# Weight parts at other byte offsets in a fp32 decoder trunk: a ring of six places and a cycle of eight wide offsets

## The chip, the cores and the metric

The kernel runs on one core of one Trainium2 chip. Its metric is the device time of one execution in microseconds (us). A comparison of this kernel with another one can tell a difference of about 2% from no change.

The engines are named as the profile names them: PE multiplies matrices (PEld is its loading of the stationary operand, LDWEIGHTS), ACT and DVE work elementwise, POOL here mostly issues DMAs that add to their target, and SP issues the other DMAs.

## The reference

One sequence of 512 tokens with 1024 features goes through two layers, in fp32. Layer 0 mixes with a gated DeltaNet (6 heads of 128, in chunks), layer 1 with sliding-window attention (12 query heads, 2 shared key/value heads); both attend to 256 memory tokens as well. Each layer ends in a SwiGLU of width 2816:

```
x = x + concat([mix_out, mem_o]) @ w_out[layer]
x = x + swiglu(rms_norm(x, ln_ffn[layer]), w_gate_up[layer], w_down[layer])

def swiglu(h, w_gate_up, w_down):
    gu = h @ w_gate_up
    return (jax.nn.silu(gu[..., :D_FF]) * gu[..., D_FF:]) @ w_down
```

After the last layer comes one more RMS norm. Most of the arithmetic is in these matrix products: the input projections, w_out, w_gate_up and w_down.

## The kernel before

**Three products for one.** Every fp32 operand of a large product is split into a high part (rounded to the matmul's fp32r form by a copy on ACT) and a low part (the rest, by a subtraction on DVE): `split`, lines 176 to 178. Then `mm3` (lines 206 to 212) issues three matmuls for each 128 rows of contraction: high weight by high activation, high weight by low activation, low weight by high activation. The weight is the stationary operand, the activation the moving one, with 512 or 256 columns (tokens).

**Where the parts lie.** `parts` (lines 190 and 191) takes a pair of tiles, `whi` for the high and `wlo` for the low part, from a pool with three buffers of each. A tile has 1024 + 64 elements of 4 bytes in each partition; SPARE is the 64. `weight` (lines 193 to 204) loads a raw weight (`wraw`) and puts both parts at element 0 of such a pair; these are the *wide* weights, up to 1024 elements long. In the built program all these tiles and all activations begin at the same remainder modulo 256 bytes, so a part's offset in its tile is also its offset from the moving operand, modulo 256.

**The quarters and the ring.** Most of w_gate_up is multiplied with seven products of half size in place of eight (a Strassen-like scheme). `quarters` (lines 1005 to 1052) does one such group for a pair of column tiles; each call of `product` (lines 1020 to 1025) takes one of the seven half weights (512 elements), splits it on ACT and DVE, and multiplies it with 256 columns by 4 times `mm3`, which is 12 matmuls. `held` copies a finished sum out of its PSUM bank (the `fs` tiles, 256 elements on ACT); sums of finished products go to `fu` and `fg` tiles on DVE. The half weights live in a *ring* of six places (lines 893 to 900): three pairs of tiles, each cut into two halves of 512 elements, and used in turn, so the two halves of one pair are neighbours in the order of use. Before the change the halves lie at elements 16 to 527 and 528 to 1039 of the tile (SHIFT is 16). There are two stretches of ten quarters in each layer's `ffn`, 70 products each, four stretches in all; `places` is emptied at the start of each, so each begins a new round of the ring with its first product.

**What orders the work.** The order on each engine is set when the program is built, by a scheduler that follows the dependences between tiles. A split into a place of the ring waits until the matmuls that read what it overwrites are done; where two areas of a tile overlap in a single element, that counts as the same data. Each engine then works through its instructions in that order, and waits on semaphores.

Of the kernel before, what the change touches and what calls it, by code (L numbers as in the profile page):

```python
# [19 lines left out]
T = 512  # L20
# [7 lines left out]
FT = DFF // P  # L28
EPS = 1e-6
LINE = 64  # L30
SHIFT, SPARE = 16, 64
NEG = -1e30
BASE = 32
NB = P // BASE
# [54 lines left out]
class Builder:  # L89
    def __init__(self, tc, a):  # L90
        self.tc, self.nc, self.a = tc, tc.nc, a
        self.n = 0
        self.table, self.table_ins, self.table_users = None, None, []


# [97 lines left out]
    def weight(self, src, eng=None, raw=None, parts=1, pool=None, tags=("whi", "wlo"), bufs=3):  # L193

        raw = self.load(src) if raw is None else raw
        n = raw.shape[1]
        if pool is None:
            hi, lo = (x[:, :n] for x in self.parts())
        else:
            hi, lo = (self.t(pool, [P, D], F32R, t, bufs)[:, :n] for t in tags)  # L200
        for i in range(parts):
            s = slice(i * n // parts, (i + 1) * n // parts)
            self.split(raw[:, s], hi[:, s], lo[:, s], eng or self.weng)
        return hi, lo
# [665 lines left out]
    def ffn(self, fp, xp, layer, h, apool, rope=False):  # L870
# [3 lines left out]
        acts, sums, open_pairs, places = [], [], [], []  # L874
# [18 lines left out]
        def ring():  # L893

            if not places:
                for _ in range(3):
                    two = self.parts()
                    places.extend(tuple(x[:, SHIFT + i * T:SHIFT + (i + 1) * T] for x in two) for i in range(2))
            places.append(places.pop(0))
            return places[-1]  # L900

        def begin(f, up, by, tag, bufs, then):

            o = [self.t(fp, [P, T], F32, tag, bufs) for _ in range(2)]
            steps = self.quarters(fp, [col(f + i, up) for i in range(2)], sums, by, o, ring)
            next(steps)
            end()
            next(steps)
            open_pairs.append((steps, then, o))
            return o  # L910
# [13 lines left out]
        for f0, half in ((0, 12), (12, 10)):  # L924
# [16 lines left out]
            for m in range(tail):  # L941
                ps = self.bank("pj")
                for j in (0, 6):
                    n = min(6, half - j)
# [8 lines left out]
        if tail < KD:  # L953
# [9 lines left out]
            for t in parts:  # L963
                acc = self.acc[:, t]
                for m in range(tail, KD):
# [3 lines left out]
                    x = self.x[m][:, t]  # L969
# [301 lines left out]
```

## Time and profile before

| | |
|---|---|
| time, median of 2 runs | 1159.43 us (1157.88 to 1160.98) |
| time of the profiled execution | 1156.72 us |
| its span, first to last instruction | 1155.0 us |
| PE busy | 1131.5 us (98%) |
| DVE busy | 842.6 us (73%) |
| ACT busy | 631.7 us (55%) |
| POOL busy | 86.0 us (7%) |
| granted PE clock | 0.998 of full |

The span is what the profile's views divide up; 1.7 us of the execution's time lie around it. Matmuls overlap each other: a matmul of 256 columns shows a duration of about 0.28 us, but the next one begins about 0.12 us later. What counts for the time is this distance from one start to the next, here called the pitch, and not the duration.

### The profile page before, as it was taken

Reading aid. Unit: us, or ns where it says so; the run is one execution under the profiler, and the core shown is the slowest. Engines: PE = TensorE matmul, PEld = TensorE weight load, DVE = VectorE, ACT = ScalarE, POOL = GpSimd, SP = SyncE. Lnnn points to the kernel's source line nnn. Section 1 sums busy time; section 2 is a strip of 40 time slices with the busy share of each in tenths; the row PEclk is TensorE's granted clock in tenths of the full one; section 3 lists DMA queues with packets and bytes.
Section 4 is the critical chain, followed back from the end, with each engine's and each line's share of the span. In section 5 each row is a group of like instructions: output and inputs, shape, how many; then the busy total and the mean of one; then the engine's idle time right before and its main releaser. Section 6 shows DMA issues by size and latency. Waiting matters only on the chain.

```text
span 1155.0 us, 19665 instructions
## 1 busy us (share of the span) xinstructions
PE 1131.5 (98%) x7476; PEld 992.9 (86%) x7476; DVE 842.6 (73%) x1587; ACT 631.7 (55%) x1271; POOL 86.0 (7%) x97
## 2 busy tenths in 40 slices
PE   7999999999999999999999999999999999999996
PEld 6888778887899998899998777777899988999986
DVE  6754877767789987389866767859799843898754
ACT  7579563366556652256654547675566522566533
POOL 0310000000101100011100000010011100111000
PEclk9999999999999999999999999999999999999999
DMA  8434342225657744567723421144477733577232
GB/s 309 133 106 117 113 103 98 92 92 165 168 139 190 188 123 126 154 147 188 178 70 104 137 73 38 51 107 126 110 188 191 183 109 105 141 183 188 72 94 94
DMA packets 73971, 152.83 MB, mean 132 GB/s; under 512 B 17756, under 2 KB 18420, under 8 KB 73876
## 3 DMA queue, kind: packets, MB, share of 16 engines
q1 hardware_dynamic: 62356, 130.59, 36.2%
q0 software_dynamic: 11520, 20.98, 11.7%
q8 instruction: 59, 0.97, 0.4%
q14 instruction: 36, 0.29, 0.1%
HBM read 144.58 MB, written 6.96 MB: 131 GB/s over the span
## 4 chain that ended last, share of the span: by engine, by line
PE 85%; DVE 8%; ACT 3%; DMA 3%; issue 1%; SPq 0%; DVEq 0%; ACTq 0%
PE pj L154 40%; PE g L154 38%; PE sc L154 5%; DVE wlo L161 2%; ACT sm L142 1%; PE pt L158 1%; DMA wraw<-in_wout 1%; PE qk L154 1%; ACT whi L148 1%; PE g L158 1%; DVE l L164 1%; DMA wraw<-in_wmk 1%; DVE btmp L161 1%; DVE stats L778 1%; DVE big L161 1%
## 5 line engine op out<-in xcount | busy, mean ns | idle before, releaser
L148 ACT ACTIVATE whi<-wraw 128x512 fp32r<-128x512 f32 (+2 forms) x331 | 244.1, 745 | 256.1 <-PE pj L154 155.9
L161 DVE TENSOR_TENSOR wlo<-wraw,whi 128x512 fp32r<-128x512 f32 (+2 forms) x331 | 274.6, 839 | 104.6 <-ACT whi L148 98.6
L154 PE MATMUL pj<-h,whi 128*128 128x512 f32 (+1 forms) x676 | 266.5, 396 | 0.0
L154 PE MATMUL pj<-l,whi 128*128 128x512 f32 (+1 forms) x676 | 264.9, 392 | 0.5 <-DVE l L164 0.4
L154 PE MATMUL pj<-h,wlo 128*128 128x512 f32 (+1 forms) x676 | 264.3, 391 | 0.0
L154 PE MATMUL g<-T,whi 128*128 128x256 f32 x1280 | 230.2, 281 | 0.0
L154 PEld LDWEIGHTS g<-T,whi 128*128 128x128 f32 x1280 | 197.5, 190 | 1.7 <-DVE fu L164 1.7
L154 PE MATMUL g<-T,wlo 128*128 128x256 f32 x640 | 179.9, 281 | 0.0
L154 PEld LDWEIGHTS pj<-h,whi 128*128 128x128 f32 x676 | 126.8, 188 | 29.2 <-issue 3.6
L154 PEld LDWEIGHTS pj<-l,whi 128*128 128x128 f32 x676 | 127.2, 188 | 27.8 <-issue 1.8
L154 PEld LDWEIGHTS pj<-h,wlo 128*128 128x128 f32 x676 | 127.1, 188 | 25.6 <-issue 0.8
L154 PE MATMUL g<-l,whi 128*128 128x256 f32 (+1 forms) x508 | 146.1, 288 | 0.0
L154 PE MATMUL g<-h,whi 128*128 128x256 f32 (+1 forms) x508 | 146.0, 287 | 0.0
L154 PE MATMUL g<-h,wlo 128*128 128x256 f32 (+1 forms) x508 | 145.9, 287 | 0.0
L154 PEld LDWEIGHTS g<-T,wlo 128*128 128x128 f32 x640 | 120.2, 188 | 0.0
L154 PEld LDWEIGHTS g<-l,whi 128*128 128x128 f32 x508 | 97.4, 192 | 1.4 <-issue 0.2
L154 PEld LDWEIGHTS g<-h,whi 128*128 128x128 f32 x508 | 95.4, 188 | 1.2
L154 PEld LDWEIGHTS g<-h,wlo 128*128 128x128 f32 x508 | 95.4, 188 | 1.0
L1014 POOL DMA_DIRECT2D ws<-in_wgu x40 | 35.4, 884 | 700.9 <-ACT sq L151 244.5
L148 ACT ACTIVATE whi<-ws 128x512 fp32r<-128x512 f32 x80 | 50.5, 631 | 51.3 <-PE g L154 42.1
L161 DVE TENSOR_TENSOR fu<-pj,rstd 128x512 f32<-128x512 f32 (+1 forms) x34 | 22.4, 660 | 54.3 <-PE pj L154 54.3
L161 DVE TENSOR_TENSOR wlo<-ws,whi 128x512 fp32r<-128x512 f32 x80 | 54.9, 686 | 6.9 <-ACT whi L148 6.8
(345 smaller groups left out, 1617.2 us busy)
## 6 DMA issues: line engine op xcount, KB each, us to landing
wraw<-in_wgu SPq DMA_DIRECT2D x48, 512.0 KB, 4.3
ws<-in_wgu SPq DMA_DIRECT2D x80, 256.0 KB, 3.7
ws<-in_wgu POOLq DMA_DIRECT2D x80, 256.0 KB, 4.8
wraw<-in_wdn SPq DMA_DIRECT2D x48, 384.0 KB, 3.1
wraw<-in_win SPq DMA_DIRECT2D x26, 512.0 KB, 3.6
wraw<-in_wgu SPq DMA_DIRECT2D x40, 256.0 KB, 4.2
wraw<-in_wout SPq DMA_DIRECT2D x16, 512.0 KB, 3.7
wraw<-in_wdn SPq DMA_DIRECT2D x16, 256.0 KB, 2.7
```

The source lines that it names most:

```text
L142: ins = self.nc.scalar.activation(out, in_, func, **kw).ins
L148: self.copied = self.nc.scalar.activation(out, in_, AF.Copy, **kw).ins
L154: return self.nc.tensor.matmul(out, lhsT, rhs, start=start, stop=stop, skip_group_check=more).ins
L158: return self.nc.tensor.transpose(out, in_, self.ident[:k, :k]).ins
L161: return eng.tensor_tensor(out=out, in0=a, in1=b, op=op).ins
L164: self.nc.vector.scalar_tensor_tensor(out=out, in0=in0, scalar=scalar, in1=in1, op0=op0, op1=op1)
L778: nc.vector.tensor_reduce(out=mx[:, i:i + 2], in_=ps[b], op=ALU.max, axis=AX.X)
L1014: nc.gpsimd.dma_start(s1, a22, accum_op=ALU.add)
```

## The change

The ring's six places get six different offsets in place of 16 elements for all, and a wide weight gets one of eight offsets in turn in place of 0. Nothing else is changed: the same splits, matmuls and DMAs are there, in the same number, on tiles of the same size at the same addresses.

```
-SHIFT, SPARE = 16, 64
+NARROW, WIDE, SPARE = ((56, 44), (36, 54), (50, 58)), (0, 52, 44, 40, 36, 20, 12, 28), 64
...
         if pool is None:
-            hi, lo = (x[:, :n] for x in self.parts())
+            o = WIDE[self.wide % len(WIDE)]
+            self.wide += 1
+            hi, lo = (x[:, o:o + n] for x in self.parts())
...
-                for _ in range(3):
+                for shifts in NARROW:
                     two = self.parts()
-                    places.extend(tuple(x[:, SHIFT + i * T:SHIFT + (i + 1) * T] for x in two) for i in range(2))
+                    places.extend(tuple(x[:, o + i * T:o + (i + 1) * T] for x in two) for i, o in enumerate(shifts))
```

The offsets are in elements. 56, 44, 36, 54, 50 and 58 elements are 224, 176, 144, 216, 200 and 232 bytes; counted up to the next multiple of 256 they leave the 32, 80, 112, 40, 56 and 24 of the change's description, and the wide ones (0, 208, 176, 160, 144, 80, 48 and 112 bytes from the tile's start) leave 0, 48, 80, 96, 112, 176, 208 and 144. So no offset of the ring stays as it was (64 bytes), and a wide weight stays at 0 in one use of eight.

The two halves of the first pair now lie at elements 56 to 567 and 44 + 512 = 556 to 1067: elements 556 to 567 belong to both. The second pair lies at 36 to 547 and 566 to 1077, the third at 50 to 561 and 570 to 1081, without a common element. In what follows, place 0 and place 1 are the two halves of the first pair.

This changes the order of the program in the four stretches of quarters. The first product of a stretch on PE, before (`whi_651` and `wlo_652` are the first pair of the ring, `whi_653` and `wlo_654` the second; `h` and `T` tiles are activations, `g` tiles are PSUM banks; the first two rows end the product of place 0, the rest begins that of place 1):

```order
L154 MATMUL g_648_3287<-l_571_2907,whi_651_3290 128x256
L154 MATMUL g_648_3287<-h_570_2906,wlo_652_3291 128x256
L154 MATMUL g_650_3289<-T_610_3125,whi_651_3290 128x256 [waits Activation_49]
L154 MATMUL g_650_3289<-T_611_3126,whi_651_3290 128x256
L154 MATMUL g_650_3289<-T_610_3125,wlo_652_3291 128x256 [waits DVE_49]
L154 MATMUL g_650_3289<-T_620_3173,whi_651_3290 128x256
```

The same place on PE now:

```order
L155 MATMUL g_648_3287<-l_571_2907,whi_651_3290 128x256
L155 MATMUL g_648_3287<-h_570_2906,wlo_652_3291 128x256
L155 MATMUL g_650_3289<-T_610_3125,whi_651_3290 128x256 [waits Activation_49]
L155 MATMUL g_650_3289<-T_611_3126,whi_651_3290 128x256
L155 MATMUL g_649_3288<-h_577_2945,whi_653_3292 128x256
L155 MATMUL g_648_3287<-T_610_3125,whi_653_3292 128x256 [waits Activation_49]
L155 MATMUL g_648_3287<-T_611_3126,whi_653_3292 128x256
L155 MATMUL g_648_3287<-T_610_3125,wlo_654_3293 128x256 [waits DVE_49]
L155 MATMUL g_650_3289<-T_610_3125,wlo_652_3291 128x256 [waits DVE_49]
```

Between the first two matmuls of place 1 and its third stand four matmuls of the second pair. The first matmul of place 1 directly follows the last of place 0 in both orders.

On ACT, the splits into the ring at the start of the same stretch, before (`whi_655` is the third pair; the rows between them belong to gates and sums of the same stage):

```order
L148 ACTIVATE whi_651_3290<-wraw_644_3277 128x512 [waits DMAHW3_49,PE_49]
L148 ACTIVATE T_640_3269<-fu_638_3262 128x512 [waits DVE_49]
L148 ACTIVATE whi_651_3290<-ws_645_3279 128x512 [waits DMASW0_49]
L142 ACTIVATE fg_616_3162<-fg_616_3162 128x512 [waits DVE_49]
L148 ACTIVATE T_640_3269<-fu_639_3263 128x512 [waits DVE_49]
L148 ACTIVATE whi_653_3292<-wraw_644_3277 128x512 [waits DVE_49,PE_49]
```

The same splits now, from the split into the second pair on to the next use of place 0:

```order
L149 ACTIVATE whi_653_3292<-wraw_644_3277 128x512 [waits DVE_49,PE_49]
L149 ACTIVATE whi_653_3292<-wraw_644_3277 128x512
L143 ACTIVATE fg_626_3210<-fg_626_3210 128x512 [waits DVE_49]
L149 ACTIVATE whi_655_3294<-wraw_644_3277 128x512 [waits DVE_49,PE_49]
L149 ACTIVATE whi_655_3294<-ws_646_3280 128x512 [waits DMASW1_49]
L143 ACTIVATE fg_636_3258<-fg_636_3258 128x512 [waits DVE_49]
L149 ACTIVATE whi_651_3290<-ws_645_3279 128x512 [waits DMASW0_49,PE_49,Activation_49]
L149 ACTIVATE fs_657_3310<-g_648_3287 128x256 [waits PE_49]
L149 ACTIVATE whi_651_3290<-wraw_662_3395 128x512 [waits DMAHW4_49,DVE_49,PE_49]
```

The split into place 1 (from `ws_645`) stood third in the ring's order and waited for its DMA alone. Now it stands behind the splits into the other four places, and waits for PE: the matmul it waits for is the last that reads the high part of place 0. The next split into place 0 waits for PE and DVE again.

Later in the stretch the scheduler puts more matmuls between place 0 and place 1. On PE in the second round (`g_668` is the bank of place 1's product; the first row ends the product of place 0):

```order
L155 MATMUL g_666_3405<-h_570_2906,wlo_652_3291 128x256
L155 MATMUL g_648_3287<-T_610_3125,whi_653_3292 128x256 [waits DVE_49]
L155 MATMUL g_648_3287<-T_611_3126,whi_653_3292 128x256
L155 MATMUL g_648_3287<-T_610_3125,wlo_654_3293 128x256
L155 MATMUL g_648_3287<-T_620_3173,whi_653_3292 128x256
L155 MATMUL g_648_3287<-T_621_3174,whi_653_3292 128x256
L155 MATMUL g_648_3287<-T_620_3173,wlo_654_3293 128x256
L155 MATMUL g_668_3407<-T_610_3125,whi_651_3290 128x256 [waits Activation_49]
L155 MATMUL g_668_3407<-T_611_3126,whi_651_3290 128x256
```

Six matmuls of the next product were moved ahead of place 1's. In the third round the piece is shorter, and begins with a wait of its own: `g_666` is the bank of the product that has just ended, and the next matmul writes it again.

```order
L155 MATMUL g_666_3405<-T_640_3269,wlo_652_3291 128x256
L155 MATMUL g_666_3405<-T_610_3125,whi_653_3292 128x256 [waits DVE_49]
L155 MATMUL g_666_3405<-T_611_3126,whi_653_3292 128x256
L155 MATMUL g_682_3540<-h_549_2790,whi_651_3290 128x256 [waits Activation_49]
L155 MATMUL g_682_3540<-l_550_2791,whi_651_3290 128x256
```

The DVE instruction waited for is the `fu` sum that reads the bank `g_666` after the row above it. Counted over the program, the split into place 1 comes 48 times, 12 in each stretch. Between the matmul that releases it and the first matmul that needs it stand 1 other matmul in 8 of them, 3 in 8 (these have the bank's wait as well), 7 in 30 and 11 in 2. Before the change a split into the ring that waits for PE has at least 30, and in most cases 60, matmuls between the two.

More of the change, by code (lines that the diff above doesn't have):

```diff
@@ L92, in __init__ @@
         self.n = 0
+        self.wide = 0
         self.table, self.table_ins, self.table_users = None, None, []
```

## The prediction

> **What bounds the kernel now.** I read the page's head and its chain first, then the chain in order of time, then the busy times by stretch.
>
> ```profile
> span 1155.0 us, 19665 instructions
> PE 1131.5 (98%) x7476; PEld 992.9 (86%) x7476; DVE 842.6 (73%) x1587; ACT 631.7 (55%) x1271; POOL 86.0 (7%) x97
> PE 85%; DVE 8%; ACT 3%; DMA 3%; issue 1%; SPq 0%; DVEq 0%; ACTq 0%
> PE pj L154 40%; PE g L154 38%; PE sc L154 5%; DVE wlo L161 2%; ACT sm L142 1%; PE pt L158 1%; DMA wraw<-in_wout 1%; PE qk L154 1%; ACT whi L148 1%; PE g L158 1%; DVE l L164 1%; DMA wraw<-in_wmk 1%; DVE btmp L161 1%; DVE stats L778 1%; DVE big L161 1%
> ```
>
> PE holds 85% of the chain. The `g` share is mostly the quarters, the `pj` share the products with wide weights. In order of time the chain shows the four stretches as single pieces, with wide weights between them:
>
> ```profile
> 332.73 97.52 PE g L154 x828
> 497.16 97.52 PE g L154 x828
> 825.07 97.52 PE g L154 x828
> 989.50 97.52 PE g L154 x828
> 432.99 64.17 PE pj L154 x283
> 1139.06 5.89 PE pj L154 x49
> ```
>
> Each stretch is 97.52 us of matmuls without a gap, for 828 of its 840 (70 products of 12; the last product comes after other work). So the **pitch in the ring** is 97.52 / 828 = 0.1178 us. For wide weights it is 64.17 / 283 = 0.2267 us with 512 columns and 5.89 / 49 = 0.1202 us with 256 (the last row, the halved end of the kernel, at offset 0). From the last two, a column costs (0.2267 - 0.1202) / 256 = 0.000416 us, 256 columns cost 0.1065 and 512 cost 0.2130. What a matmul costs beside its columns is therefore 0.0137 us at offset 0 and 0.0113 us at the ring's 64 bytes.
>
> The other engines in a stretch (PE, PEld, DVE, ACT, POOL, granted clock, DMA share, GB/s):
>
> ```profile
> 332.73:430.25 97.52, 97.52 (x829) 97.52 (x829) 86.70 (x156) 61.22 (x118) 13.49 (x16) 1.00 0.68 169
> 497.16:594.68 97.52, 97.52 (x830) 97.52 (x829) 85.43 (x153) 61.80 (x118) 12.94 (x15) 1.00 0.65 156
> ```
>
> DVE is busy for 89% of it and ACT for 63%, and both keep ahead of PE only because the ring lets them split up to five products early.
>
> **The change, part by part.** *The ring's overlap.* Places 0 and 1 share 12 elements, so the split into place 1 cannot begin before PE has read place 0, the product just before. That is a new wait, 48 times. Its price goes by the path from PE over ACT back to PE. The durations:
>
> ```profile
> L148 ACT ACTIVATE whi<-wraw 128x512 fp32r<-128x512 f32 x217 | 133.9, 628 | 87.2 <-PE g L154 40.7 <-PE pj L154 36.1 <-ACT fs L148 2.5
> L161 DVE TENSOR_TENSOR wlo<-wraw,whi 128x512 fp32r<-128x512 f32 x217 | 146.5, 689 | 33.1 <-ACT whi L148 27.6
> L164 DVE SCALAR_TENSOR_TENSOR fu<-g,fs x22: 416/417/419, 341.5 to 1087.5; 128x256 f32<-128x256 f32 x22
> ```
>
> How long an engine takes to notice PE, and PE to notice it, stands in two places of the timeline:
>
> ```profile
> 347.88 0.28 PE L154 MATMUL g<-l,whi 128*128 128x256 f32 x1
> 348.00 0.28 PE L154 MATMUL g<-h,wlo 128*128 128x256 f32 x1
> 348.25 0.63 ACT L148 ACTIVATE whi<-wraw 128x512 fp32r<-128x512 f32 x1 [0.28 <-PE g L154]
> ...
> 11.36 1.23 DVE L161 TENSOR_TENSOR wlo<-wraw,whi 128x1024 fp32r<-128x1024 f32 x1 [0.88 <-ACT whi L148]
> 12.64 0.39 PE L154 MATMUL pj<-mh,wlo 128*128 128x256 f32 x1 [0.76 <-DVE wlo L161]
> 12.86 0.28 PE L154 MATMUL pj<-mh,whi 128*128 128x256 f32 x1
> ```
>
> In the first the last high read of a product starts at 347.88 and the split that it releases at 348.25: 0.37 us. In the second DVE ends at 12.59 and PE starts at 12.64: 0.05 us; the matmul behind comes 0.22 later where 0.12 is usual, so a restart costs 0.10 more. A released split therefore costs 0.37 + 0.63 + 0.05 + 0.10 = **1.15 us** from the start of the releasing matmul, and what PE has between takes a pitch for each matmul and one more. By the counts in the order:
> - 1 matmul between (8 times): 1.15 - 2 x 0.118 = 0.91 us each, 7.3 us.
> - 3 between (8 times): the split would cost 1.15 - 0.47, but the bank's wait comes before it: 0.37 + 0.42 + 0.05 + 0.10 = 0.94 us after the product's last matmul, less one pitch, 0.82 us, which covers the split. 6.6 us.
> - 7 between (30 times): 1.15 - 8 x 0.118 = 0.21 us, 6.3 us.
> - 11 between (2 times): nothing.
>
> That is 20.2 us if ACT and DVE are free each time. They are not. Behind the waiting split on ACT stand the `fs` copy of the product that has just ended, the splits into the third pair and place 0, and the `h` and `fg` work; on DVE `wlo` of place 1 stands behind the sums and raw additions. I followed four of the seven-matmul cases. In one, two sums and a raw addition hold the low split until 1.30 us, and its third matmul comes 0.18 late (restart with it). In two, ACT is still on a copy and a split at 0.37 and begins at 0.59, 0.22 late. In one the low part is needed after 5 matmuls and costs a restart, 0.12. Mean 0.19; with DVE at 89% I take 0.25 for 38 of the cases, 9.5 us. Sum: **30 us**. Below, the 20.2 stand alone; above, twice the lateness makes 40. The next use of place 0 waits for place 1's first two high reads and has 21 to 27 matmuls (2.5 to 3.2 us) of cover, against 1.15 for ACT and about 0.7 more for DVE, so it costs nothing while DVE is no more than 0.6 us late.
>
> The `ws` loads that POOL adds up wait for the same splits. They land in 4.8 us and are two quarters (2 x 7 x 12 x 0.118 = 19.8 us) ahead, so a shift of 1 us hides there.
>
> ```profile
> ws<-in_wgu POOLq DMA_DIRECT2D x80, 256.0 KB, 4.8
> ```
>
> *The new offsets on ACT and DVE.* Nothing, by the nearest rows: DVE works as fast on rows that begin 4, 8 or 12 bytes off as on aligned ones.
>
> ```profile
> L164 DVE SCALAR_TENSOR_TENSOR qv<-pj,gains,qv 128x511 f32<-128x511 f32 x12 | 9.0, 746 | 2.7 <-ACT qv L148 2.4
> L164 DVE SCALAR_TENSOR_TENSOR qv<-pj,gains,qv 128x509 f32<-128x509 f32 x12 | 8.9, 742 | 0.1
> L164 DVE SCALAR_TENSOR_TENSOR l<-x,gains,h 128x512 fp32r<-128x512 f32 x32 | 23.5, 747 | 1.5 <-ACT h L148 1.5
> ```
>
> *The new offsets on PE.* No row shows a weight at these offsets; two rows show that an offset can matter (0.0137 at 0, 0.0113 at 64 bytes). For the ring the bounds are the whole 0.0113 gained, 3360 x 0.0113 = 38 us, and a return to 0.0137, 3360 x 0.0024 = 8 us lost. I take 0: the nearest row is the ring's own. For wide weights the chain's `pj` share is 0.40 x 1155 / 0.2267 = 2040 matmuls, seven eighths of them moved, 1785. Bounds: 0.0137 gained, 24 us, and as much lost as the ring's two values differ, 4 us. I take the one step that the rows show, 1785 x 0.0024 = **4 us gained**.
>
> The Trainium skill, SBUF — State Buffer, section "SBUF: two separate sides", says that PE has its own ports and never waits on another engine there. By that rule no offset of a weight part changes the pitch through other engines' accesses, and the gain would be 0 and the sum 30. The two pitches above differ in nothing I can see but the offset, so the trace does not settle it.
>
> **The sum.** 30 - 4 = 26 us. On the profiled execution, 1156.7 + 26 = 1182.7 us. The median of the runs is 2.7 us higher, so I forecast **1185 us**.
>
> **The rivals.**
> - *The pitch falls enough to pay for most of the stalls* (not slower by what can be measured, about 2%, 23 us). Place: every matmul with a weight of the ring or a moved wide weight. The two measured offsets speak for it, and that nothing but the offset seems to separate them; against it, that two points say nothing of 13 others. It decides from a saving of 7 us on; a saving of half the wide bound and a little in the ring, 17 us, gives 1159.4 + 30 - 17 = 1172 us.
> - *The pitch falls to little more than the columns* in ring and wide weights: 62 us saved, 1159.4 + 30 - 62 = 1127 us, faster by over 2% from a saving of 53 us on. A price only from a page: the Trainium skill, TensorE: Matmul & The Clock Gate, section "Wait — 56ns, not 53.3ns?", states 2.5 ns beside the columns for each warm matmul. By it the estimate is 3360 x 0.0088 + 1785 x 0.0112, 50 us saved, 1140 us; this trace shows 11 and 14 ns, not 2.5.
> - *DVE becomes the bound of the stretches.* It has 10.8 us to spare in each and now stands idle while ACT splits place 1, up to 1 us in 12 events. If that idle time can't be used and the sums fall behind, each stretch lasts as long as DVE's work plus its old and new idle time, 86.7 + 10.8 + 12: 12 us more than before in place of 7.5, and with the ring back at 0.0137 this gives 1159.4 + 48 + 8 = 1215 us.
> - *The change does not do what it says*, since one use in eight stays at 0: that is in the count above.
>
> **How the numbers follow.** The forecast's case (stalls of 24 to 40 us, pitch within a few us) 0.60; five sixths of it lie above the 2% line of 1182.6 us. The first rival 0.26, the second 0.04, the third 0.10. Slower by over 2%: 0.50 + 0.10 = 0.60. Within 2%: 0.10 + 0.26 = 0.36. Faster by over 2%: 0.04. The range leaves out the second rival and the ends of the others. Low end: stalls of 20.2, 15 saved, 1159.4 + 5 = 1165 us. High end: stalls of 40, 8 lost in the ring, 1159.4 + 48 = 1207 us.
>
> **What would show it.** The four stretches, now 97.52 us each, should last about 105 us, and the chain in them should break into pieces of about 60 to 72 matmuls with ACT `whi` and DVE `fu` or `wlo` between. PE `g` should wait for ACT `whi` some 46 times, for 0.2 to 0.9 us. The pitch within the pieces should be 0.118 us, and the piece of 283 matmuls should take between 63.5 and 64.2 us. DVE and ACT rows should stay at 689 and 628 ns. I am wrong if the stretches keep their length (the order hides the wait), or if the wide pieces change by more than 3 us in 64 either way (the offset is a matter of PE alone, and larger than I took it).

## The result and the profile after

The changed kernel takes 1205.65 us (median of 2 runs, 1205.51 and 1205.80) against 1159.43 us before: a ratio of 1.040, 95% interval 1.038 to 1.042. That is 46 us slower, where 26 us were forecast; the time lies inside the range (1165 to 1207), near its upper end.

The page of the changed kernel begins so (the span, the busy times, and the chain by engine):

```profile
span 1204.0 us, 19620 instructions
PE 1159.9 (96%) x7476; PEld 1002.4 (83%) x7476; DVE 842.9 (70%) x1587; ACT 630.2 (52%) x1271; POOL 86.3 (7%) x97
PE 81%; DVE 8%; DMA 4%; ACT 4%; issue 2%; SPq 0%; DVEq 0%; ACTq 0%
```

DVE and ACT do the same work in the same time as before (842.6 and 631.7 us), so their instructions did not become longer. The span grew by 49.0 us and PE's busy time by 28.4 us only: the rest is time in which PE stands. The busy times by stretch, with the four stretches of quarters first and then the wide piece behind the first of them (PE, PEld, DVE, ACT, POOL, granted clock, DMA share, GB/s):

```profile
334.86:443.65 108.79, 102.87 (x830) 100.53 (x829) 86.25 (x155) 60.54 (x117) 13.85 (x16) 0.98 0.61 151
511.85:620.18 108.33, 103.78 (x845) 101.13 (x844) 86.97 (x156) 61.94 (x119) 13.87 (x16) 1.00 0.59 147
852.67:959.73 107.06, 101.56 (x830) 99.14 (x829) 85.74 (x153) 60.43 (x117) 17.41 (x20) 1.00 0.67 164
1027.94:1137.61 109.67, 105.05 (x844) 102.58 (x844) 87.05 (x156) 61.93 (x119) 13.84 (x16) 0.98 0.58 145
446.01:511.85 65.84, 65.84 (x287) 53.34 (x286) 37.04 (x57) 15.61 (x21) 3.51 (x4) 1.00 0.46 126
```

The second and the fourth of these windows hold some 15 matmuls more than the first. From the first to the last of its 840 matmuls a stretch takes 108.2 to 111.0 us now and took 100.0 to 100.2 before; the four together are 37.8 us longer, about 9.4 us each, and what lies outside them is 11.2 us longer. The wide piece shows the second part: 65.84 us, at a clock of 1.00, for the 284 matmuls that the chain counts in it (the window touches 287), 0.2318 us each, against 0.2267 before.

In the stretches PE now waits. The groups of waits of PE and of its weight loads (what waits, for whom: us in total, times, the longest):

```profile
PEld g L155 <- ACT whi L149: 17.6, 21, 2.9
PE g L155 <- ACT whi L149: 13.6, 11, 2.7
PE g L155 <- DVE fu L165: 6.8, 8, 0.8
```

The waits for `whi` are in part the same events, seen once at the weight load and once at the matmul. The eight for `fu` are the eight bank waits of the forecast. But the longest wait for `whi` is 2.7 us, where the forecast had 0.9 at most. The chain in order of time shows what stands ahead of it (start, duration, what; the pieces follow each other directly):

```profile
385.41 0.03 DVE fg L162
385.44 7.29 DMA wraw<-in_wgu
...
392.81 0.63 ACT whi L149
393.44 0.27 ACT fs L149
393.71 1.05 ACT whi L149 x2
394.76 0.04 issue
394.81 1.35 PE g L155 x8
```

The raw weight `wraw` of a quarter has two buffers. DVE gives one back at 385.41, its next load takes 7.29 us, ACT can split it only then, and a copy and one more split stand in ACT's row between this split and the one that PE needs. Such a load stands ahead of five of the six stalls over 1.1 us (a stall is counted here as the time from one matmul to the next beyond the pitch). Ahead of the sixth, of 2.35 us in the fourth stretch, ACT's split of an activation `h` waits for a DVE sum, and the split that PE needs stands behind it.

The load is the seventh of its kind in the stretch. The first row below is its issue in the kernel before; the other two are from the changed kernel, the load of another raw tile (`last` in `quarters`) and this one:

```profile
374.56 0.33 SPq L187 DMA_DIRECT2D wraw<-in_wgu  x1
...
384.76 0.33 SPq L1020 DMA_DIRECT2D wraw<-in_wgu  x1
385.44 0.33 SPq L188 DMA_DIRECT2D wraw<-in_wgu  x1
```

Before, PE had started 357 matmuls of the stretch when this load was issued; now it has started 396. The load comes 39 matmuls (4.6 us) later against PE's row. It also follows the other load by 0.7 us, where the nearest such load before came 3.8 us behind it (378.40), and takes longer than the 4.1 us of the median.

### The profile page after: what moved, and what is told of

Read it like the earlier page. It is cut to its first block, busy times and chain, and to the rows that moved or that the text cites. A ratio compares the mean times of both kernels' runs of the same rounds, so it can differ in the third digit from the quotient of the medians.

```text
span 1204.0 us, 19620 instructions
## 1 busy us (share of the span) xinstructions
PE 1159.9 (96%) x7476; PEld 1002.4 (83%) x7476; DVE 842.9 (70%) x1587; ACT 630.2 (52%) x1271; POOL 86.3 (7%) x97
## 4 chain that ended last, share of the span: by engine, by line
PE 81%; DVE 8%; DMA 4%; ACT 4%; issue 2%; SPq 0%; DVEq 0%; ACTq 0%
PE pj L155 41%; PE g L155 32%; PE sc L155 6%; DVE wlo L162 3%; DMA wraw<-in_wgu 2%; ACT whi L149 2%; DMA wraw<-in_wout 1%; ACT sm L143 1%; PE pt L159 1%; PE qk L155 1%; PE g L159 1%; DVE l L165 1%; DVE fu L165 1%; DMA wraw<-in_wmk 1%; DVE stats L781 1%
## 5 line engine op out<-in xcount | busy, mean ns | idle before, releaser
L155 PE MATMUL pj<-h,whi 128*128 128x512 f32 (+1 forms) x676 | 269.2, 400 | 0.5 <-ACT h L149 0.5
L155 PE MATMUL g<-T,whi 128*128 128x256 f32 x1280 | 239.8, 285 | 14.7 <-ACT whi L149 7.7
L155 PEld LDWEIGHTS pj<-h,wlo 128*128 128x128 f32 x676 | 127.1, 188 | 28.4 <-issue 0.8
```

The source lines that it names most:

```text
L155: return self.nc.tensor.matmul(out, lhsT, rhs, start=start, stop=stop, skip_group_check=more).ins
```

## The experiments

Every run is compared with runs of the kernel before on the same chip.

### Which part costs what: the overlap, the wide offsets, the ring's offsets

**No overlap.** The two offsets of the first pair change places, so that the six ring offsets and the wide cycle stay in use, and no element is shared:

```
-NARROW = ((56, 44), (36, 54), (50, 58))
+NARROW = ((44, 56), (36, 54), (50, 58))
```

> The changed kernel with the first pair's two offsets exchanged (44 and 56 elements), so that its halves lie at elements 44 to 555 and 568 to 1079 and share none; the same six ring offsets and the same wide cycle are used. Theory (the shared elements cause the whole growth of the four stretches, the wide offsets cost about 10 us elsewhere): stretches back at 97.5 us each, no wait of PE g for ACT whi in them, wide pieces still 65.8 us, total 1169 to 1171 us. Rival A (the six ring offsets themselves make the stretches longer): stretches stay at 107 to 110 us, total 1195 to 1206 us. Rival B (the stalls also made the wide pieces longer, over clock or late loads): stretches 97.5, wide pieces 64.2, total 1159 to 1161 us.

Measured: 1170.44 us, ratio 1.009 (1.007 to 1.011). Its chain, in order of time:

```profile
336.64 98.35 PE g L155 x828
437.77 65.61 PE pj L155 x283
```

The stretch is one piece of 98.35 us again, and PE `g` waits for ACT `whi` nowhere in it. So the shared elements alone cost 46.2 - 10.7 = **35.5 us**. The 98.35 us are 0.8 us more than before the change: without stalls the six offsets cost 3.3 us over the four stretches, against none forecast. The wide piece stays at 65.6, so its length has nothing to do with the stalls.

**Wide weights at 0.** The ring keeps its overlap:

```
-WIDE = (0, 52, 44, 40, 36, 20, 12, 28)
+WIDE = (0,)
```

> The changed kernel with all wide weights back at element 0; the ring with its shared elements stays. Theory (wide offsets cost about 10 us by themselves): the piece between two stretches goes from 65.8 back to 64.2 us, the stretches stay at 107 to 110 us, total 1195 to 1198 us. Rival B (wide offsets cost nothing, the wide pieces were longer because of the stalls): 65.8 stays, total 1205 us.

Measured: 1194.95 us, 1.031 (1.029 to 1.033). In its chain the wide piece is nearly back at its old length:

```profile
444.22 64.43 PE pj L155 x284
```

and in its groups of waits those of the ring stay:

```profile
PE g L155 <- ACT whi L149: 12.0, 9, 2.7
```

The wide cycle costs 46.2 - 35.2 = **11 us** in this kernel. With the run above, the two parts account for the whole change.

**The overlap alone.** One ring offset is changed and nothing else; place 0 moves to 28 elements and so runs 12 elements into place 1:

```
+NARROW, WIDE = ((28, 16), (16, 16), (16, 16)), (0,)
```

> The overlap alone: place 0 at 28 elements (112 bytes), the other five places at 16, so that places 0 and 1 share 12 elements as in the changed kernel; all wide weights at element 0. Theory (the overlap's wait costs 38 us and nothing else matters in the ring): stretches 107 to 110 us each, total 1196 to 1199 us, wide piece 64.2 us. Rival A (the offsets, not the overlap): stretches near 97.5 to 99 us, total 1159 to 1165 us.

Measured: 1195.18 us, 1.032 (1.028 to 1.035), the same as with all six offsets changed (1194.95). The waits are much the same as well:

```profile
PE g L155 <- ACT whi L149: 13.6, 12, 2.6
PE g L155 <- DVE fu L165: 6.5, 8, 0.8
```

**The wide cycle alone.** The ring lies at 64 bytes in all places, as before the change:

```
+NARROW = ((16, 16), (16, 16), (16, 16))
 WIDE = (0, 52, 44, 40, 36, 20, 12, 28)
```

> The wide cycle alone: all six places of the ring back at 16 elements (64 bytes), no shared element, the wide weights in turn at the eight new offsets. Theory (wide offsets cost about 10 us, ring offsets without overlap nothing): 1169 to 1171 us, the same as with the six new ring offsets and no overlap; wide piece 65.8 us. Rival A (the ring's offsets cost by themselves): this kernel is faster than the one with six new offsets and no overlap. Rival B (wide offsets cost nothing): 1159 us.

Measured: 1153.05 us, 0.994 (0.992 to 0.996): *faster* than before, 17 us under the theory and 6 under rival B. Rival A, which gave no size, has the order right: this kernel is faster than the one with six new offsets and no overlap. The chain:

```profile
335.52 93.85 PE g L155 x828
432.17 65.62 PE pj L155 x283
497.79 88.42 PE g L155 x780
```

The wide piece is as long as with the cycle anywhere else. But the stretch takes 93.85 us where it took 97.52, a pitch of 0.1133 us in place of 0.1178, in all four stretches. In a stretch this kernel has the same instructions on the same addresses as the kernel before; the only difference lies in the wide weights that run ahead of it. So it is not the ring's own offset, as rival A has it, and the next runs went for what else it is.

### What sets the pitch

**A step ahead of the stretch.** The kernel before, in which only the last wide weight ahead of each stretch lies at 80 bytes (84 of its matmuls: 24 ahead of the first and the third stretch, 18 ahead of the second and the fourth):

```
+            self.step = 20 if f == 3 else 0
             ps = self.project(col(f, 0), h, "pj")
...
+                    self.step = 20 if f0 == 0 and (m, j) == (tail - 1, 6) else 0
                     w = down(m, j, n)
```

> The kernel before (ring at 64 bytes, wide at 0, no overlap) with one edit: only the one or two wide weights that run directly ahead of each of the four stretches lie at 80 bytes (20 elements). Theory (the same ring of the same offsets has two steady pitches, 0.1177 and 0.1133 us, and the matmuls ahead of it decide which, for as long as no gap breaks the row): all four stretches go to 93.9 us, total 1159.5 - 15 = 1145 us. Rival (the ring was faster in the run with shifted wide weights for another reason, for example because the shifted wide weights lie in the tile elsewhere while the ring runs): stretches stay at 97.5 us, total 1159 to 1161 us.

Measured: 1151.81 us, 0.994 (0.992 to 0.995). Two stretches of four changed, the second and the fourth:

```profile
333.47 97.52 PE g L155 x828
433.75 64.27 PE pj L155 x283
498.02 88.42 PE g L155 x780
```

88.42 / 780 = 0.1134 us. So a ring of the same offsets has **two steady pitches**, 0.1178 and 0.1134 us. A stretch shows one of them from its first products to its last, and the matmuls ahead of it decide which. The theory's 1145 us was wrong, because one moved weight ahead of the first and third stretch is not enough, though it is ahead of the second and fourth.

**More steps.** Two moved weights ahead of the first and third stretch, or all four gate weights there; ahead of the second and fourth as in the run above:

```
+            self.step = {2: 36, 3: 20}.get(f, 0)       (two)
+            self.step = (44, 40, 36, 20)[f]            (four)
```

> The kernel before with the wide weights directly ahead of each stretch moved: ahead of the first and third stretch the last gate weight to 80 bytes and the one before it to 144, ahead of the second and fourth the last weight to 80 bytes. Theory (the matmuls ahead decide the ring's pitch; 144 and then 80 bytes ran ahead of the first stretch where it had 0.1133 us): all four stretches 93.9 us, total 1159 - 14 = 1145 us. Rival (more of the history than two weights counts): stretches one and three stay at 97.5, total 1152 us.

> As the run with two steps, but all four gate weights ahead of the first and third stretch are moved, to 176, 160, 144 and 80 bytes. Theory (the matmuls ahead decide): all four stretches 93.9 us; two more moved weights of 24 matmuls in each layer cost 2 x 48 x 0.005 = 0.5 us more than two steps if those reach the fast state too, total 1145 to 1146 us. Rival (what decides lies elsewhere than in the matmuls directly ahead): 1152 us or 1159 us.

Measured: 1152.74 us with two (0.994, 0.993 to 0.996), and **1146.04 us with four (0.989, 0.987 to 0.990)**. With four all stretches have the lower pitch; its first two of them:

```profile
333.94 93.85 PE g L155 x828
494.88 88.42 PE g L155 x780
```

With two, the first and third stretch stay at the higher one, as the rival had it. The two runs already differ in the weight at 144 bytes, the last but one ahead of the first stretch. The first row of its 24 matmuls and the first row behind them, of the run with two steps:

```profile
322.69 0.39 PE L155 MATMUL pj<-h,whi 128*128 128x512 f32 x1
328.14 0.39 PE L155 MATMUL pj<-h,whi 128*128 128x512 f32 x1
```

and of the run with four:

```profile
322.62 0.39 PE L155 MATMUL pj<-h,whi 128*128 128x512 f32 x1
328.21 0.40 PE L155 MATMUL pj<-h,whi 128*128 128x512 f32 x1
```

5.45 / 24 = 0.2271 us and 5.59 / 24 = 0.2329: the same weight at the same offset, with a different pitch, by whether the one before it had already left the low one. So the wide pitch, too, goes by what ran before, not by the offset alone. The last weight ahead of the stretch, at 80 bytes, takes 0.232 us a matmul in both runs, and yet the stretches behind it differ: the pitch directly ahead does not decide by itself. The version with four steps is faster than both kernels; its 1.1% is less than the 2% that a comparison can tell from no change, but the interval lies below 1 and the trace shows where the time goes.

**All weights at 64 bytes.** To see whether an offset has a price of its own:

```
+NARROW, WIDE = ((16, 16), (16, 16), (16, 16)), (16,)
```

> No overlap; every weight part, wide and ring, at 64 bytes (16 elements). Theory (a weight offset has a pitch of its own, and the ring's 64 bytes gives 0.0113 us beside the columns): wide pitch 0.2130 + 0.0113 = 0.2243 us, the piece between two stretches 63.6 us, ring as before at 0.1177, total 1159 - 5 = 1154 us. Rival A (any wide offset but 0 costs 3 to 6 ns, as the eight did): wide pitch 0.230 to 0.233, piece 65.5 us, total 1167 to 1170 us with the ring at 0.1177. Rival B (the ring's pitch depends on what ran ahead of it, as the run with the ring at 64 bytes behind shifted wide weights suggests, 0.1133 there): stretches 93.9 us in place of 97.5, 15 us less than by either of the others.

Measured: 1166.80 us, 1.007 (1.004 to 1.009). The theory fell; it is rival A, with the stretches of rival B in one place only:

```profile
336.04 93.85 PE g L155 x828
432.69 66.03 PE pj L155 x283
498.71 97.52 PE g L155 x828
```

At 64 bytes a wide matmul takes 66.03 / 283 = 0.2333 us, more than at 0, though a ring matmul takes less there (0.1178 or 0.1134) than at 0, as the next run shows.

**All weights at 0.**

```
+NARROW, WIDE = ((0, 0), (0, 0), (0, 0)), (0,)
```

> All weight parts at the moving operand's own offset (0), ring and wide. Theory (distance 0 is the fastest for 512 columns, 0.2267 us, but for 256 columns it shows 0.1197, against 0.1177 at 64 bytes): stretches 828 x 0.1197 = 99.1 us, total 1159 + 4 x 1.6 = 1166 us. Rival (distance 0 is best for any width, and 0.1197 came from the few places where it stood): stretches 93.9 to 97 us, total 1145 to 1157 us.

Measured: 1166.08 us, 1.006 (1.004 to 1.008), as the theory had it. Its first stretch:

```profile
334.13 99.35 PE g L155 x828
```

99.35 / 828 = 0.1200 us. Of the two offsets 0 and 64 bytes, the faster one for 256 columns is the slower one for 512.

**Offset from what?** The kernel before, with a pad of 64 bytes at the beginning of the constants. The weight tiles and the `h` and `l` activations move together; the `T` tiles and `ac8` to `ac11` stay:

```
+            cp.tile([P, 16], F32, name="pad")
             self.load_constants(cp)
```

> The kernel before with a 64-byte pad ahead of its constants: the weight tiles, the h and l activations and the first eight pairs of the down products' activations all move by 64 bytes; the T activations and the pairs ac8 to ac11 stay where they are. Theory (the pitch goes by the distance between weight part and moving operand modulo 256): wide products with h, l and the first eight pairs keep 0.2267 us, those with ac8 to ac11 (now at a distance of 64 bytes) change by some ns; in the ring the products with h and l and those with T part in their pitch. Rival A (it goes by the weight part's own address): all wide products change alike. Rival B (neither; only the steps from one offset to another count): nothing changes by more than 1 ns but the state of the ring.

Measured: 1158.01 us, ratio 1.000 (0.999 to 1.001). Four rows of one of its wide products: the first with `ac8`, the first behind the 12 with `ac8` to `ac11`, and, further on, one with `h` and the next one with `ac8`, 18 matmuls later:

```profile
436.89 0.39 PE L154 MATMUL pj<-ac8h,whi 128*128 128x512 f32 x1
...
439.69 0.39 PE L154 MATMUL pj<-h,whi 128*128 128x512 f32 x1
...
441.07 0.39 PE L154 MATMUL pj<-h,whi 128*128 128x512 f32 x1
...
445.15 0.39 PE L154 MATMUL pj<-ac8h,whi 128*128 128x512 f32 x1
```

2.80 / 12 = 0.2333 us with the activations that stayed, 4.08 / 18 = 0.2267 with those that moved along. Without the pad both have 0.2267. The weight lies 64 bytes further in both, so it is the **distance between weight part and moving operand** that counts and not the weight's own address, as the theory had it; a distance of 64 bytes costs the same 0.2333 as in the run with all weights at 64 bytes. In the ring the products with `h` and `l` average 0.1145 us and those with `T` 0.1189 here, against 0.1178 for both without the pad. Each stretch is 0.6 us shorter, the products with `ac8` to `ac11` are longer, and the total stays the same.

### What makes the stalls longer than forecast

**Raw weights loaded once.** The changed kernel, with the load of a quarter's raw weight left out in all but the first two quarters of a stretch. The later quarters split the same two tiles again, as the sums left them, so the kernel leaves out those weights and computes other products; the `ws` and `last` loads stay:

```
-        a1 = self.load(src[0])
+        if len(ring.raws) < 2:
+            ring.raws.append(self.load(src[0]))
+        else:
+            ring.raws.append(ring.raws[-2])
+        a1 = ring.raws[-1]
```

> The changed kernel, overlap and offsets kept, with part of the work left out: in each stretch the raw weight tile wraw of a quarter is loaded only for the first two quarters; the later ones take the same two tiles again as the sums left them, so that no split waits for a raw weight load in the stretch (the ws and last loads stay). PE's order is the same. Theory (the stalls of 1.1 to 2.9 us come from late splits that give the raw tiles back late, so that their loads land late, and the clock falls behind the longest of them): the six long stalls go down to the 0.2 to 1.1 us of their class, stretches go from 107 to 110 us to 105 to 107 us, total 1193 to 1198 us. Rival (the loads are late but something else holds the splits just as long): 1204 to 1206 us.

Measured: 1193.63 us, 1.030 (1.028 to 1.032). Its first stretch, in the columns of the stretches above:

```profile
334.98:439.41 104.43, 101.29 (x829) 99.09 (x829) 86.26 (x155) 60.65 (x117) 13.82 (x16) 1.00 0.52 117
```

and its waits:

```profile
PE g L155 <- DVE fu L165: 6.8, 8, 0.8
PE g L155 <- ACT whi L149: 5.7, 8, 0.8
```

The stretch is 4.4 us shorter, the waits for `whi` are eight of at most 0.8 us, which are the forecast's cases with one matmul between, and the clock stays at 1.00. None of the six long stalls is left, the sixth included. So 46.2 - 34.8 = **11.4 us** of the change come from raw loads that land late and from what follows them. The loads that are left out also take traffic off the DMA queues: the other loads of the stretches land 0.4 to 0.6 us sooner by their medians. So part of the 11.4 may come from that; the run doesn't part the two.

What follows them is the clock. After the longest stall of the changed kernel, of the stretches from 391.80 on (columns as above, the granted clock is the third from the end):

```profile
391.80:394.80 3.00, 0.30 (x3) 0.10 (x1) 1.29 (x2) 1.94 (x4) 0.79 (x1) 1.00 0.27 84
394.80:396.50 1.70, 1.69 (x11) 1.68 (x12) 1.70 (x5) 1.22 (x3) 0.08 (x1) 0.77 0.54 70
396.50:398.90 2.40, 2.40 (x13) 2.40 (x13) 1.47 (x3) 0.95 (x3) 0.00 (x0) 0.50 0.90 195
```

PE stands for 2.7 us, starts again, and 0.9 us later its clock falls to half for some 3 us: 13 matmuls in 2.40 us, 0.185 each, where 0.118 is usual. It happens twice in the changed kernel, behind its two longest stalls.

## Why the prediction was right, and where it was not

**The direction and the main cause were right.** The overlap of 12 elements makes the split into place 1 wait for PE's reads of place 0, and that one wait gives 35.5 of the 46 us. It does so with one ring offset changed as well as with six (the overlap alone: 1195 us) and vanishes when the same offsets change places.

**The term for the released splits, 20.2 us, was right in kind and 4 to 7 us low.** In the run without late raw loads, the intervals from one matmul to the next in the four stretches, as far as they are longer than the pitch of 0.118 us, add up to 26.8 us; by the medians it is 35.5 - 11.4 = 24.1. Two of its waits, the last matmul ahead of each and the one that waits:

```profile
336.10 0.28 PE L155 MATMUL g<-h,wlo 128*128 128x256 f32 x1
337.04 0.50 PE L155 MATMUL g<-T,whi 128*128 128x256 f32 x2 [0.66 <-ACT whi L149]
...
354.30 0.28 PE L155 MATMUL g<-T,wlo 128*128 128x256 f32 x1
355.43 0.50 PE L155 MATMUL g<-T,whi 128*128 128x256 f32 x2 [0.85 <-DVE fu L165]
```

The first is a case with one matmul between. Four of these cost 0.82 beyond the pitch and 0.10 for the restart, 0.92 in sum where 0.91 was worked out; the other four cost 0.93 and 0.10. The second is a bank wait: the eight cost 1.01 and 0.10, where I had 0.82 in all; the cases with seven cost 0.2 to 0.3, where I had 0.21 and then 0.25 more.

**The term for lateness was wrong in kind, and close in sum by luck.** I put 9.5 us on ACT and DVE being behind in 38 cases, a quarter of a microsecond each. That is not what happened: most cases have no such lateness. Six long stalls carry what the trace has beyond the released splits, and only one of them shows ACT and DVE late without a load ahead. The step that failed is "a shift of 1 us hides there". I worked it out for the `ws` loads, which stand two quarters ahead, and left out that the delayed splits read the two buffers of `wraw` as well. A late split gives one back late, its load (7.29 us in the chain above) lands late, and the next splits wait for it: PE stands 1.1 to 2.9 us each time. Nor is the shift 1 us: the load of that chain is issued 39 matmuls, 4.6 us, later against PE's row, right behind another one. What the run without these loads saves is 11.4 us, the fall of the clock included, and the forecast had none of it. Of the sum of 30, the stretches therefore show 38.

**The term for the wide offsets had the wrong sign.** I took "the one step that the rows show, 1785 x 0.0024 = 4 us gained", from two pitches of 256 columns, and carried it to 512. It measured 7 to 11 us lost: 10.7 in the run without overlap, less the 3.3 of its ring, and 11 by taking the cycle out of the changed kernel. For 512 columns the distance 0 is the fastest that any run shows (0.2267), and 64 bytes are slow (0.2333), while for 256 columns it is the other way round (0.1200 and 0.1178 or 0.1134). The bound I gave on the losing side, 4 us, was too narrow for the same reason. With both terms at these sizes the sum would have been 45 to 49 us, against a span that grew by 49.0.

The Trainium skill, SBUF — State Buffer, section "SBUF: two separate sides", says that PE never waits on another engine there. No run here tests that. The run with the pad shows that the distance between PE's own two operands counts (0.2333 against 0.2267); the rule has no word on that, and the gain of 0 that the prediction worked out from it was not the measured loss either.

**"For the ring I take 0" was right for this kernel.** Two rows between two stalls:

```profile
389.00 0.28 PE L155 MATMUL g<-T,wlo 128*128 128x256 f32 x1
391.11 0.28 PE L155 MATMUL g<-T,wlo 128*128 128x256 f32 x1
```

They are 18 matmuls apart, 0.1172 us each. But it was right for no good reason: the value I started from, 0.1178 at 64 bytes, is one of two that the same ring shows, and which of them it is hangs on the matmuls ahead. Between the stalls of the changed kernel all four stretches average 0.118. Without the overlap the six offsets give 98.35 / 828 = 0.1188.

**The rivals.** A pitch that falls enough to pay for the stalls did not occur in this kernel. The idea that there is a lower one was sound, though: 0.1134 in the ring is worth 15 us, and comes from other offsets *ahead* of the ring, not in it. DVE as the bound (1215 us) is near the result in time and not in mechanism: its 86.25 us in a stretch of 108.79 leave it idle for a fifth. That the change doesn't do what it says is out.

**What was to be seen.** Stretches of about 105 us: they take 107 to 110, and 104.4 without the late raw loads. Pieces of 60 to 72 matmuls with ACT `whi` and DVE between: there are fewer and longer ones, since the cases with seven matmuls between cost only 0.2 us and mostly don't break the chain. Some 46 waits of PE `g` for ACT `whi`: the view names 11, and 21 of the weight load. ACT and DVE rows as before: yes, 630 and 690 ns against 628 and 689. A wide piece of 63.5 to 64.2 us: no, 65.84.

## What to carry to other kernels

Two areas that share a few elements are one area to whatever orders the work; so look whether cut-out places in a tile really end where the next begins, and when a split is delayed, follow every buffer that it gives back, the raw weight's and not only the next operand's. A matmul pitch read from one profile belongs to its number of columns, to the distance between its two operands and to what ran before it, and must not be carried from one of these to another. Where long rows of equal matmuls run without a gap, it is worth trying other offsets for the few matmuls ahead of them: here that gave 13 us in the best run, for 228 moved matmuls.

## What the runs showed of the hardware

- A row of equal matmuls can have two steady pitches, with the same instructions and addresses: 0.1178 and 0.1134 us for 256 columns. It keeps the one it begins with over all of the 828 matmuls; with 512 columns at 144 bytes it was 0.2271 and 0.2329. That the history decides is shown; by what mechanism is not, and no run tried it.
- The pitch goes by the distance between weight part and moving operand: 0.2267 us at 0 and 0.2333 at 64 bytes with 512 columns, and still 0.2267 when both move by 64 bytes together. The Trainium skill, TensorE: Matmul & The Clock Gate, section "Wait — 56ns, not 53.3ns?", gives one fixed 2.5 ns beside the columns. Here what stands beside them, by the 0.000416 us a column of the prediction, is 7 to 14 ns for 256 columns and 14 to 20 for 512.
- In the changed kernel the clock fell to 0.50 after PE had stood idle for 2.7 us, 0.9 us after it had started again. It did so too 1.3 us after an idle gap of 2.2 us, and not behind one of 1.7. The Trainium skill, TensorE: Matmul & The Clock Gate, section "Part 1: The HAM clock gate (the "warmup" mystery)", states an idle window of about 3.4 us for the fall. This trace shows it behind shorter gaps.
